# A longer weave of the gate stage, samples first in the query and key projections, and a later place for the attention output transposes

## The chip, the core and the metric

The kernel runs on one NeuronCore of one Trainium2 chip. The metric is the device time of one execution, in microseconds (us). Before the change three executions took 1855.73 us (median), 1855.55 us and 1857.43 us. The engines have short names here: PE is TensorE's matmul side and PEld its weight loads, DVE is VectorE, ACT is ScalarE, POOL is GpSimd, and SP is the engine that issues most DMAs.

## What is computed

The reference runs a small encoder of two layers over two batches that share their weights: a prompt of 512 tokens and a sample of 256 tokens, each 1024 wide.

```python
def _mixer(x, w_in, ...):
    aq, ak, av, lq, lk, lv, lo, lg = _split_cols(x @ w_in)
    att = _diff_attention(aq, ak, av, lam)            # 4 heads, two softmaxes each, ALiBi bias
    att = _head_rmsnorm(att, att_g) * (1.0 - lam_init)
    gates = lg + gate_bias                            # 16 columns: input and forget gates, two directions
    h_f = _mlstm_direction(q, k, v, ig_f, lf_f)       # chunks of 128 tokens, cumulative sums and running maxima
    h_b = flip(_mlstm_direction(flip(q), flip(k), flip(v), flip(ig_b), flip(lf_b)))
    lstm = sigmoid(lo) * _head_rmsnorm(h_f + h_b, lstm_g)
    return concatenate([att, lstm]) @ w_out
# each layer: x = LN1(ALPHA*x + mixer(x));  x = LN2(ALPHA*x + conv_gated_ffn(x))
```

## The kernel before

Both batches lie side by side as T = 768 tokens, in NT = 6 tiles of 128; tiles 0 and 1 are the sample (SB = 256 tokens), tiles 2 to 5 the prompt. A product in 32-bit accuracy is made of three passes: each operand is split into a high part and a rest, and high x high, high x rest and rest x high are summed in PSUM. So a projection of one token tile (`tok_major`) is 8 blocks of 128 inputs times three passes, 24 matmuls. The tiles of one projection are called after it: `av0` to `av5` (attention values), `lv0` to `lv5` (LSTM values), `lo0` to `lo5` (output gate).

Queries and keys of one head are made the other way round, features on the partitions (`feat_major`): 24 weight pieces, each used for the 256 sample columns (into the bank `aqkB`) and the 512 prompt columns (into `aqkA`). `att_in` does it twice per head, first for the query (`aqkA00` for head 0), then for the key (`aqkA01`). Both use the two halves of one sample bank (`aqkB0`). ACT and DVE then split the query into `sQ` and the key into `sK` and `kL`. `att` makes the scores (`s`), the two softmaxes and their difference (`tp`), its transpose (`aT`), the product with the values (`u`), and at the end of a batch the normalised output `ao` and its transpose `aoT`.

`gates` is a chain of small steps: logarithms of the gates, a transpose (`gT`), scans along the tokens on DVE (lines 483 to 487), maxima and exponentials, a small matmul that spreads a factor over the partitions (`aB`, line 517), and transposes back (`colT`). It also writes two scratch arrays to memory, from which `lstm_decay` later loads `pt` (512 KB, line 570) and `qet` by DMA. In `pt` DVE adds a mask (line 572) and ACT takes exponentials (line 574).

Weights come in pieces of 256 KB over the queue of SP (line 140). There are 6 buffers for them as they arrive, and 12 slots for the split form `wh`, `wl`, made by ACT (line 171) and DVE (line 172). A slot comes free when the last matmul that reads it is done, and a load waits until an older piece has been split.

The stages are generators. `weave` takes steps from several of them in turn, in the ratio of the numbers given with them, and so writes the program's order. Each instruction gets a priority from its place in that order; `prio(n)` shifts it, a negative n to a later place. A list scheduler then places each engine's instructions by priority, data and free buffers. In hardware each engine takes its list in order. `islice(lv, 1)` takes the first token tile from a projection and leaves the rest for later.

Of the kernel before, what the change touches and what calls it, by code (L numbers as in the profile page):

```python
# [20 lines left out]
SA, SB = 512, 256  # L21
T = SA + SB
# [24 lines left out]
PR_A = 0  # L47
PR_L = 0
PR_LO = 10
# [2 lines left out]
PR_S = -20  # L52
PR_T = -20
PR_E = 50
PR_CONV1 = -100
PR_CONV2 = -100
SBUFS = 2
# [148 lines left out]
def trunk(ctx, nc, tc, d, o, depth=DEPTH):  # L206
    V, S, G, PE = nc.vector, nc.scalar, nc.gpsimd, nc.tensor
# [11 lines left out]
    @contextmanager  # L219
    def prio(offset):  # L220

        tc.cur_priority -= offset
        yield
        tc.cur_priority += offset

    def P(tag, name):
        return pp.tile([128, 512], F32, tag=tag, name=name, bufs=banks[tag])

    actA = cp.tile([128, 8, 2, T], F32R, name="actA")
# [17 lines left out]
    for i in range(2):  # L247
        k = 4 * i
# [70 lines left out]
    ident = cp.tile([128, 128], F32, name="ident")  # L319
# [19 lines left out]
    PASSES = ((0, 0), (0, 1), (1, 0))  # L339

    def tok_major(t, blocks, ps, cols):

        for k, (_, h, l) in enumerate(blocks):
            for i, (a, b) in enumerate(PASSES):
                PE.matmul(ps, xh(k, t, a), (h, l)[b][:, cols], start=k + i == 0, stop=k == 7 and i == 2)  # L345

    def feat_major(blocks, psA, psB):

        n = 0
        for k in range(8):  # L350
            _, h, l = blocks[k // 4]
            for a, b in PASSES:
                w = (h, l)[a][:, (k % 4) * 128:(k % 4 + 1) * 128]
                PE.matmul(psB, w, actA[:, k, b, 0:SB], start=n == 0, stop=n == 23)  # L354
                PE.matmul(psA, w, actA[:, k, b, SB:T], start=n == 0, stop=n == 23)  # L355
                n += 1

    def transposed_split(src, name, tag, hi, lo):

# [8 lines left out]
    for l in range(depth):  # L368
# [3 lines left out]
        av = ra.tile([128, NT, 512], F32, name="av")  # L372
# [24 lines left out]
        def dense(tag, evac):  # L397
            units = [W.take() for _ in range(8)]
            for t in range(NT):
                p = P("d", f"{tag}{t}")  # L400
                tok_major(t, units, p, slice(0, 512))
                evac(t, p)
                yield
            W.done(*units)
# [23 lines left out]
        def gates():  # L428
# [38 lines left out]
            t2 = gp.tile([128, T], F32, name="t2")  # L467
            mpe = gp.tile([64, 2, 6], F32, name="mpe")
            ae = gp.tile([64, 6], F32, name="ae")
            for c0, c1 in ((0, 4), (4, 6)):  # L470
                ps = P(TAG_GT, f"gT{c0}")
                n = (c1 - c0) * 128
                for t in range(c0, c1):
                    PE.transpose(ps[:, (t - c0) * 128:(t - c0 + 1) * 128], gs[:, t].rearrange("p a b c -> p (a b c)"), ident)
                S.copy(ig[:, c0 * 128:c1 * 128], ps[0:64, :n])
                V.tensor_copy(lf[:, c0 * 128:c1 * 128], ps[64:128, :n])
# [35 lines left out]
            V.tensor_tensor(out=v6(t2[64:128]), in0=v6(t1[0:64]), in1=me.unsqueeze(2).to_broadcast([64, 6, 128]), op=ALU.subtract)  # L512
            V.tensor_tensor(out=ae, in0=mp, in1=me, op=ALU.subtract)
            S.activation(ae, ae, AF.Exp)
            ps = P(TAG_GT, "aB")
            for i in range(4):
                PE.matmul(ps[:, i * 6:(i + 1) * 6], sel[:, i, :], ae, start=True, stop=True)
# [2 lines left out]
            for c0, c1 in ((0, 4), (4, 6)):  # L520
                for ti, src in ((0, t1), (1, t2)):
                    ps = P(TAG_COLT[ti], f"colT{c0}{ti}")
# [169 lines left out]
        def att(h):  # L692
            slope = 2.0 ** (-8.0 * (h + 1) / 4)
            for s0, s1 in SEQ_ORDER[h]:
                nq = s1 - s0
                n = nq * 128
                keys = slice(s0 * 128, s1 * 128)
                pu = P("u", f"u{h}{s0}")
                ssu = sm.tile([128, 4], F32, tag="ssu", name=f"ssu{h}{s0}")
                sm0 = sm.tile([128, 4], F32, tag="sm0", name=f"sm0{h}{s0}")  # L700
                for qt in range(nq):
                    qtok = slice((s0 + qt) * 128, (s0 + qt + 1) * 128)
                    tp = ra.tile([128, 2, 512], F32, tag="tp", name=f"tp{h}{s0}{qt}", bufs=2)
                    mn = sm.tile([128, 2], F32, tag="mn", name=f"mn{h}{s0}{qt}")
                    cc = sm.tile([128, 1], F32, tag="cc", name=f"cc{h}{s0}{qt}")
                    for c in range(2):
                        ps = P("s", f"s{h}{s0}{qt}{c}")
                        PE.matmul(ps[:, :n], sQ[:, c, qtok], sK[:, c, keys], start=True, stop=False)
                        PE.matmul(ps[:, :n], sQ[:, c, qtok], kL[:, c, keys], start=False, stop=True)
                        V.tensor_tensor_reduce(out=tp[:, c, :n], in0=ps[:, :n], in1=dneg[:, 384 - 128 * qt:384 - 128 * qt + n], scale=-slope, scalar=3e38,  # L710
                                               op0=ALU.add, op1=ALU.min, accum_out=mn[:, c:c + 1])

                    for c in range(2):
                        S.activation(tp[:, c, :n], tp[:, c, :n], AF.Exp, bias=mn[:, c:c + 1], scale=-1.0, accum_out=sm0[:, qt:qt + 1] if c == 0 else cc)
                    V.reciprocal(cc, cc)
                    V.scalar_tensor_tensor(out=cc, in0=sm0[:, qt:qt + 1], scalar=nlam[:, l:l + 1], in1=cc, op0=ALU.mult, op1=ALU.mult)
                    V.scalar_tensor_tensor(out=tp[:, 0, :n], in0=tp[:, 1, :n], scalar=cc, in1=tp[:, 0, :n], op0=ALU.mult, op1=ALU.add)
                    pa = P(TAG_AT[qt % 2], f"aT{h}{s0}{qt}")
                    for st in range(nq):
                        PE.transpose(pa[:, st * 128:(st + 1) * 128], tp[:, 0, st * 128:(st + 1) * 128], ident)  # L720
                    aT = ra.tile([128, 512], F32, tag="aT", name=f"aT{h}{s0}{qt}", bufs=2)
                    CP[E_AT[qt % 2]](aT[:, :n], pa[:, :n])
                    for st in range(nq):
                        PE.matmul(pu[:, qt * 128:(qt + 1) * 128], aT[:, st * 128:(st + 1) * 128], av[:, s0 + st, h * 128:(h + 1) * 128], start=st == 0, stop=st == nq - 1)  # L724
                    S.activation(aT[:, 0:128], pu[:, qt * 128:(qt + 1) * 128], AF.Square, accum_out=ssu[:, qt:qt + 1])
                    yield

                V.scalar_tensor_tensor(out=sm0[:, :nq], in0=sm0[:, :nq], scalar=128 * EPS, in1=sm0[:, :nq], op0=ALU.mult, op1=ALU.mult)
                V.tensor_tensor(out=ssu[:, :nq], in0=sm0[:, :nq], in1=ssu[:, :nq], op=ALU.add)
                G.tensor_tensor(out=ssu[:, :nq], in0=ssu[:, :nq], in1=mhalf[:, 0:nq], op=ALU.pow)  # L730
                ao = ra.tile([128, 512], F32, tag="aT", name=f"ao{h}{s0}", bufs=2)
                V.tensor_tensor(out=ao[:, :n].rearrange("p (a b) -> p a b", b=128), in0=pu[:, :n].rearrange("p (a b) -> p a b", b=128),
                                in1=ssu[:, :nq].unsqueeze(2).to_broadcast([128, nq, 128]), op=ALU.mult)
                pt_ = P(TAG_AOT, f"aoT{h}{s0}")
                for qt in range(nq):
                    PE.transpose(pt_[:, qt * 128:(qt + 1) * 128], ao[:, qt * 128:(qt + 1) * 128], ident)
                S.activation(av[:, s0:s1, h * 128:(h + 1) * 128], pt_[:, :n].rearrange("p (a b) -> p a b", b=128), AF.Identity, scale=again[:, l, h:h + 1])

        def weave(*gens):

            live = [[0, n, i, g, (*o, 0)[0]] for i, (g, n, *o) in enumerate(gens)]
            while live:
                e = min(live, key=lambda e: ((e[0] + 0.5) / e[1], e[2]))
                e[0] += 1
                with prio(e[4]):
                    done = next(e[3], live) is live
                if done:
                    live.remove(e)

        def chain(*gens):  # L750
            for g in gens:
                yield from g
# [3 lines left out]
            late_constants()  # L756
        G.iota(dneg, [[-1, 896]], base=384, channel_multiplier=1, allow_small_or_imprecise_dtypes=True)
        V.scalar_tensor_tensor(out=dneg, in0=dneg, scalar=-1.0, in1=dneg, op0=ALU.mult, op1=ALU.min)
        weave((gates(), 8), (dense("av", ev_av), 7))
        CPX = ExitStack()  # L760
        lc = CPX.enter_context(tc.tile_pool(name=f"lc{l}", bufs=1, reuse_waits="tile"))
        weave((att_in(0), 3))
        weave((att(0), 7, PR_A), (dense("lv", ev_lv), 7, PR_LO))
        lo = dense("lo", ev_lo)
        weave((chain(att_in(1), att(1)), AT1, PR_A), (chain(lstm_states(lc), *[lstm_out(lc, c) for c in range(OUTS)]), 4 * OUTS + 9, PR_L), *([(islice(lo, L1), L1 + W1)] if L1 else []))
        weave((chain(att_in(2), att(2)), AT2, PR_A), (chain(*[lstm_out(lc, c) for c in range(OUTS, NT)]), 4 * (NT - OUTS) + 1, PR_L), *([(islice(lo, L2), L2 + W2, PR_LO)] if L2 else []))
# [36 lines left out]
        for t in range(NT):  # L803
            nc.sync.dma_start(acc[:, t, :], xres[t * 128:(t + 1) * 128])
        W.urgency = PR_CONV1
        LN = ExitStack()
# [200 lines left out]
        for i in range(FF_EARLY):  # L1007
            with prio(PR_E):
                next(started[i])
# [88 lines left out]
```

## Time and profile before

| | us |
|---|---|
| three executions | 1855.55, 1855.73, 1857.43 |
| profiled execution | 1855.45 |
| its span, first to last instruction | 1853.7 |
| PE busy | 1804.3 |
| DVE busy | 1340.4 |
| ACT busy | 768.9 |
| POOL busy | 241.9 |

The profiled execution is 1855.45 us long, its span 1853.7 us; 1.75 us lie outside the span. PE is busy for 97% of the span, so little is to be had but from its stops and from stretches in which its clock is low. The granted clock is shown as a share of full speed: 1.00 stands for 2.4 GHz and 0.50 for 1.2 GHz; a value between is a mean over a window. A timeline row says how long an engine stood idle before it and what released it. The end of a matmul is modelled, so that rows of matmuls overlap; the step from start to start is what one costs.

### The profile page before, as it was taken

What the parts mean: (1) busy time and instruction counts of PE and PEld (TensorE: products, weight loads), DVE (VectorE), ACT (ScalarE), POOL (GpSimd) and SP (SyncE); (2) the same over time, 40 slices, a digit from 0 to 9 for tenths busy, and PEclk for the clock granted to TensorE, in tenths of its full rate; (3) what the DMA queues carried; (4) which work ended last, traced back from release to release, by engine and by line L of the source; (5) the groups of instructions that cost most, each with busy time, mean ns of one, the idle gap of its engine ahead of it and who ended that gap; (6) DMA issues with size and microseconds to landing.
All of it is one profiled execution on the core that took longest, in us unless ns stands there. A gap on an engine that the chain in (4) does not pass through costs nothing.

```text
span 1853.7 us, 26256 instructions
## 1 busy us (share of the span) xinstructions
PE 1804.3 (97%) x9692; PEld 1587.1 (86%) x9692; DVE 1340.4 (72%) x2576; ACT 768.9 (41%) x1624; POOL 241.9 (13%) x260
## 2 busy tenths in 40 slices
PE   8899999999999999999998999999999999999998
PEld 8778777789899899899897787777898998998996
DVE  5434787589887786787954457775898877877878
ACT  4344576425343343343332455672353343343340
POOL 2000111041111111110120011011411111111102
PEclk9999999999999999999999999999999999999999
DMA  6232110402322222122322121104022221221211
GB/s 190 67 79 69 35 58 24 159 18 69 92 74 69 64 74 68 64 75 86 101 96 83 42 69 52 46 25 170 2 90 80 80 79 47 80 76 51 80 63 68
DMA packets 83280, 134.95 MB, mean 73 GB/s; under 512 B 7984, under 2 KB 27056, under 8 KB 83152
## 3 DMA queue, kind: packets, MB, share of 16 engines
q1 hardware_dynamic: 82432, 132.90, 22.7%
q8 instruction: 76, 1.25, 0.3%
q14 instruction: 52, 0.43, 0.1%
q10 hardware_dynamic: 720, 0.37, 0.1%
HBM read 126.86 MB, written 6.39 MB: 72 GB/s over the span
## 4 chain that ended last, share of the span: by engine, by line
PE 78%; DVE 13%; ACT 5%; issue 2%; POOL 2%; DMA 1%; SPq 0%; DVEq 0%; ACTq 0%; POOLq 0%
PE p L921 32%; PE dn L981 16%; PE wo L877 5%; PE aqkA L355 3%; PE lv L345 3%; PE lo L345 3%; PE aqkB L354 2%; DVE wl L172 2%; PE c1a L345 2%; PE u L724 2%; PE av L345 2%; PE c1b L345 2%; PE num L618 1%; ACT wh L171 1%; PE num L614 1%
## 5 line engine op out<-in xcount | busy, mean ns | idle before, releaser
L921 PE MATMUL p<-actA,wh 128*128 128x384 f32 x1408 | 363.4, 338 | 3.2 <-DVE g L946 3.2
L171 ACT ACTIVATE wh<-raw 128x512 fp32r<-128x512 f32 (+1 forms) x348 | 215.5, 629 | 303.3 <-PE p L921 110.2
L172 DVE TENSOR_TENSOR wl<-raw,wh 128x512 fp32r<-128x512 f32 (+1 forms) x348 | 243.2, 708 | 96.9 <-ACT wh L171 96.4
L921 PE MATMUL p<-actB,wh 128*128 128x384 f32 x1056 | 270.0, 337 | 0.0
L921 PEld LDWEIGHTS p<-actA,wh 128*128 128x128 f32 x1408 | 254.7, 188 | 5.8 <-DVE g L946 3.8
L921 PE MATMUL p<-actA,wl 128*128 128x384 f32 x704 | 237.3, 337 | 0.0
L149 POOL TENSOR_TENSOR T<-raw,raw 128x512 f32<-128x512 f32 x88 | 120.5, 1371 | 837.0 <-DVE wl L172 525.7
L981 PE MATMUL dn<-wh,actB 128*128 128x512 f32 x576 | 208.8, 396 | 1.1 <-DVE acc L988 1.1
L171 ACT ACTIVATE wh<-T 128x512 fp32r<-128x512 f32 x176 | 108.4, 628 | 221.3 <-DVE acc L988 104.9
L921 PEld LDWEIGHTS p<-actB,wh 128*128 128x128 f32 x1056 | 191.3, 188 | 0.0
L981 PE MATMUL dn<-wh,ring 128*128 128x512 f32 x480 | 179.1, 396 | 1.6 <-DVE acc L988 1.6
L921 PE MATMUL p<-actB,wl 128*128 128x384 f32 x528 | 177.2, 336 | 0.0
L988 DVE TENSOR_TENSOR acc<-acc,dn 128x512 f32<-128x512 f32 x144 | 98.1, 681 | 72.0 <-PE dn L981 71.7
L172 DVE TENSOR_TENSOR wl<-T,wh 128x512 fp32r<-128x512 f32 x176 | 129.6, 748 | 22.0 <-ACT wh L171 21.9
L981 PEld LDWEIGHTS dn<-wh,actB 128*128 128x128 f32 x576 | 108.0, 188 | 29.8 <-DVE acc L988 2.8
L921 PEld LDWEIGHTS p<-actA,wl 128*128 128x128 f32 x704 | 132.2, 188 | 0.1
L877 PE MATMUL wo<-wh,actB 128*128 128x512 f32 x384 | 122.7, 396 | 0.0
L981 PE MATMUL dn<-wl,actB 128*128 128x512 f32 x288 | 113.2, 393 | 0.0
L981 PEld LDWEIGHTS dn<-wh,ring 128*128 128x128 f32 x480 | 90.0, 188 | 24.6 <-DVE acc L988 4.2
L921 PEld LDWEIGHTS p<-actB,wl 128*128 128x128 f32 x528 | 99.1, 188 | 0.0
L355 PE MATMUL aqkA<-actA,wh 128*128 128x512 f32 x256 | 98.8, 408 | 0.0
L981 PE MATMUL dn<-wl,ring 128*128 128x512 f32 x240 | 94.5, 394 | 0.0
(265 smaller groups left out, 3412.5 us busy)
## 6 DMA issues: line engine op xcount, KB each, us to landing
raw<-in_w_g_dram SPq DMA_DIRECT2D x88, 256.0 KB, 2.8
raw<-in_w_u_dram SPq DMA_DIRECT2D x88, 256.0 KB, 2.8
raw<-in_w_down_dram SPq DMA_DIRECT2D x88, 256.0 KB, 2.8
raw<-in_w_out_dram SPq DMA_DIRECT2D x32, 256.0 KB, 2.6
pt<-scr_m SPq DMA_DIRECT2D x12, 512.0 KB, 6.2
raw<-in_w_c_dram SPq DMA_DIRECT2D x16, 264.0 KB, 3.6
raw<-in_w_av_dram SPq DMA_DIRECT2D x16, 256.0 KB, 4.1
raw<-in_w_aq_dram SPq DMA_DIRECT2D x16, 256.0 KB, 3.7
```

The source lines that it names most:

```text
L149: src["engine"].tensor_tensor(out=src["tile"], in0=a, in1=b, op=ALU.subtract)
L171: self.nc.scalar.activation(h, v, AF.Identity)
L172: self.nc.vector.tensor_tensor(out=l, in0=v, in1=h.bitcast(F32), op=ALU.subtract)
L345: PE.matmul(ps, xh(k, t, a), (h, l)[b][:, cols], start=k + i == 0, stop=k == 7 and i == 2)
L354: PE.matmul(psB, w, actA[:, k, b, 0:SB], start=n == 0, stop=n == 23)
L355: PE.matmul(psA, w, actA[:, k, b, SB:T], start=n == 0, stop=n == 23)
L614: PE.matmul(pn[:, di * 256:di * 256 + 129], qet[r, di, hh // 2, :], cst[di, c][r, hh // 2, :], start=di == dirs[0], stop=False, skip_group ...
L724: PE.matmul(pu[:, qt * 128:(qt + 1) * 128], aT[:, st * 128:(st + 1) * 128], av[:, s0 + st, h * 128:(h + 1) * 128], start=st == 0, stop=st ...
L877: PE.matmul(p, actB[:, k, a, t * 128:(t + 1) * 128], units[k][1 + b], start=n + i == 0, stop=n == 7 and i == 2)
L921: PE.matmul(ps, blk[1 + a][:, k * 128:(k + 1) * 128], x[:, k, b, :], start=k + i == 0, stop=k == 3 and i == 2)
L981: PE.matmul(p, x, (wh_, wl_)[b], start=k + i == 0, stop=k == nf - 1 and i == 2)
L988: V.tensor_tensor(out=z, in0=z, in1=p, op=ALU.add)
```

## The change

The change has three parts. The gate stage gets two more places at which the weave may take another stage's step, and is woven with a longer list: the value projection, then the whole query and key projection of head 0, then the first tile of the LSTM value projection; before, it was woven with the value projection alone, and the projection of head 0 came after it. In `feat_major` all 24 matmuls of the sample columns come first and then all 24 of the prompt columns, in place of one each in turn. And the transposes `aoT` get a priority shift to a later place. The number of instructions of each kind is the same.

```diff
--- before.py
+++ after.py
@@ -52,6 +52,7 @@
 PR_S = -20
 PR_T = -20
 PR_E = 50
+PR_AO = -40
 PR_CONV1 = -100
 PR_CONV2 = -100
 SBUFS = 2
@@ -346,14 +347,14 @@
 
     def feat_major(blocks, psA, psB):
 
-        n = 0
-        for k in range(8):
-            _, h, l = blocks[k // 4]
-            for a, b in PASSES:
-                w = (h, l)[a][:, (k % 4) * 128:(k % 4 + 1) * 128]
-                PE.matmul(psB, w, actA[:, k, b, 0:SB], start=n == 0, stop=n == 23)
-                PE.matmul(psA, w, actA[:, k, b, SB:T], start=n == 0, stop=n == 23)
-                n += 1
+        for ps, tok in ((psB, slice(0, SB)), (psA, slice(SB, T))):
+            n = 0
+            for k in range(8):
+                _, h, l = blocks[k // 4]
+                for a, b in PASSES:
+                    w = (h, l)[a][:, (k % 4) * 128:(k % 4 + 1) * 128]
+                    PE.matmul(ps, w, actA[:, k, b, tok], start=n == 0, stop=n == 23)
+                    n += 1
 
     def transposed_split(src, name, tag, hi, lo):
 
@@ -467,6 +468,7 @@
             t2 = gp.tile([128, T], F32, name="t2")
             mpe = gp.tile([64, 2, 6], F32, name="mpe")
             ae = gp.tile([64, 6], F32, name="ae")
+            yield
             for c0, c1 in ((0, 4), (4, 6)):
                 ps = P(TAG_GT, f"gT{c0}")
                 n = (c1 - c0) * 128
@@ -512,6 +514,7 @@
             V.tensor_tensor(out=v6(t2[64:128]), in0=v6(t1[0:64]), in1=me.unsqueeze(2).to_broadcast([64, 6, 128]), op=ALU.subtract)
             V.tensor_tensor(out=ae, in0=mp, in1=me, op=ALU.subtract)
             S.activation(ae, ae, AF.Exp)
+            yield
             ps = P(TAG_GT, "aB")
             for i in range(4):
                 PE.matmul(ps[:, i * 6:(i + 1) * 6], sel[:, i, :], ae, start=True, stop=True)
@@ -732,8 +735,9 @@
                 V.tensor_tensor(out=ao[:, :n].rearrange("p (a b) -> p a b", b=128), in0=pu[:, :n].rearrange("p (a b) -> p a b", b=128),
                                 in1=ssu[:, :nq].unsqueeze(2).to_broadcast([128, nq, 128]), op=ALU.mult)
                 pt_ = P(TAG_AOT, f"aoT{h}{s0}")
-                for qt in range(nq):
-                    PE.transpose(pt_[:, qt * 128:(qt + 1) * 128], ao[:, qt * 128:(qt + 1) * 128], ident)
+                with prio(PR_AO):
+                    for qt in range(nq):
+                        PE.transpose(pt_[:, qt * 128:(qt + 1) * 128], ao[:, qt * 128:(qt + 1) * 128], ident)
                 S.activation(av[:, s0:s1, h * 128:(h + 1) * 128], pt_[:, :n].rearrange("p (a b) -> p a b", b=128), AF.Identity, scale=again[:, l, h:h + 1])
 
         def weave(*gens):
@@ -756,11 +760,11 @@
             late_constants()
         G.iota(dneg, [[-1, 896]], base=384, channel_multiplier=1, allow_small_or_imprecise_dtypes=True)
         V.scalar_tensor_tensor(out=dneg, in0=dneg, scalar=-1.0, in1=dneg, op0=ALU.mult, op1=ALU.min)
-        weave((gates(), 8), (dense("av", ev_av), 7))
+        lv = dense("lv", ev_lv)
+        weave((gates(), 10), (chain(dense("av", ev_av), att_in(0), islice(lv, 1)), 10))
         CPX = ExitStack()
         lc = CPX.enter_context(tc.tile_pool(name=f"lc{l}", bufs=1, reuse_waits="tile"))
-        weave((att_in(0), 3))
-        weave((att(0), 7, PR_A), (dense("lv", ev_lv), 7, PR_LO))
+        weave((att(0), 7, PR_A), (lv, 6, PR_LO))
         lo = dense("lo", ev_lo)
         weave((chain(att_in(1), att(1)), AT1, PR_A), (chain(lstm_states(lc), *[lstm_out(lc, c) for c in range(OUTS)]), 4 * OUTS + 9, PR_L), *([(islice(lo, L1), L1 + W1)] if L1 else []))
         weave((chain(att_in(2), att(2)), AT2, PR_A), (chain(*[lstm_out(lc, c) for c in range(OUTS, NT)]), 4 * (NT - OUTS) + 1, PR_L), *([(islice(lo, L2), L2 + W2, PR_LO)] if L2 else []))
```

The first place is PE in the gate stage of layer 0. The rows show the matmul `aB` with its neighbours; `av2` and `av3` are tiles of the value projection. Before:

```order
L345 MATMUL av2_784<-wl25_573,actA_70 128x512
L345 MATMUL av2_784<-wh25_572,actA_70 128x512
L345 MATMUL av2_784<-wh26_578,actA_70 128x512
L517 MATMUL aB_778<-ae_686,sel_636 128x6 x4
L345 MATMUL av2_784<-wl26_579,actA_70 128x512
L345 MATMUL av2_784<-wh26_578,actA_70 128x512
```

And now:

```order
L346 MATMUL av3_804<-wh28_590,actA_70 128x512
L346 MATMUL av3_804<-wl28_591,actA_70 128x512
L346 MATMUL av3_804<-wh28_590,actA_70 128x512
L520 MATMUL aB_830<-ae_686,sel_636 128x6 x4
L346 MATMUL av4_836<-wh21_188,actA_70 128x512
L346 MATMUL av4_836<-wl21_189,actA_70 128x512
```

Before, 64 matmuls of the value projection stood ahead of `aB` (67 in layer 1); now 96 do, in both layers.

The second place is ACT at the projection of head 0, in layer 0: `wh` is a weight split, `sQ` takes the query out of PSUM, `pt0` is the exponential on data that come by DMA, `tp` the softmax of the first scores. Before:

```order
L171 ACTIVATE wh41_1012<-raw41_926 128x512
L574 ACTIVATE pt0_1834<-pt0_1834,cols_239 128x128 x5
L678 ACTIVATE sQ_228<-aqkB0_962 64x256
L679 ACTIVATE sQ_228<-aqkB0_962 64x256
L678 ACTIVATE sQ_228<-aqkA00_963 64x512
L679 ACTIVATE sQ_228<-aqkA00_963 64x512
L171 ACTIVATE wh42_1018<-raw42_932 128x512
```

And now, first where `sQ` is made and then where `pt0` stands:

```order
L681 ACTIVATE sQ_228<-aqkB0_949 64x256
L682 ACTIVATE sQ_228<-aqkB0_949 64x256
L172 ACTIVATE wh41_999<-raw41_917 128x512
L172 ACTIVATE wh42_1005<-raw42_923 128x512
L681 ACTIVATE sQ_228<-aqkA00_950 64x512
L682 ACTIVATE sQ_228<-aqkA00_950 64x512
```

```order
L577 ACTIVATE pt0_1834<-pt0_1834,cols_239 128x128 x5
L413 COPY vaug_237<-lv0_1101 128x4x128
L577 ACTIVATE pt0_1834<-pt0_1834,cols_239 128x128
L717 ACTIVATE tp000_1135,sm000_1134<-tp000_1135,mn000_1136 128x256
L717 ACTIVATE tp000_1135,cc000_1137<-tp000_1135,mn000_1136 128x256
L577 ACTIVATE pt0_1834<-pt0_1834,cols_239 128x128 x2
L577 ACTIVATE pt1_1856<-pt1_1856,cols_239 128x128 x7
L725 COPY aT000_1154<-aT000_1151 128x256
```

The five exponentials of `pt0` stood ahead of `sQ`; now they stand behind all of `sQ` and `sK`, and ahead of the first softmax `tp000`.

The third place is DVE at the first scores of head 0, in layer 0: L710 before and L713 now reduce the scores, `kL` is the rest of the key, L572 and L575 add the mask to `pt`. Before:

```order
L710 ISA tp000_1108,mn000_1109<-s0000_1111,dneg_233 128x256
L710 ISA mn000_1109 128x1
L710 ISA tp000_1108,mn000_1109<-s0001_1115,dneg_233 128x256
L710 ISA mn000_1109 128x1
L687 TENSOR_TENSOR kL_230<-aqkA01_1032,sK_229 64x512
L688 TENSOR_TENSOR kL_230<-aqkA01_1032,sK_229 64x512
L715 RECIPROCAL cc000_1110<-cc000_1110 128x1
L716 SCALAR_TENSOR_TENSOR cc000_1110<-sm000_1107,nlam_221,cc000_1110 128x1
L717 SCALAR_TENSOR_TENSOR tp000_1108<-tp000_1108,cc000_1110 128x256
```

And now:

```order
L575 TENSOR_TENSOR pt0_1834<-pt0_1834,tri_243 128x512 x2
L713 ISA tp000_1135,mn000_1136<-s0000_1138,dneg_233 128x256
L713 ISA mn000_1136 128x1
L713 ISA tp000_1135,mn000_1136<-s0001_1142,dneg_233 128x256
L713 ISA mn000_1136 128x1
L575 TENSOR_TENSOR pt1_1856<-pt1_1856,tri_243 128x512
L718 RECIPROCAL cc000_1137<-cc000_1137 128x1
L575 TENSOR_TENSOR pt1_1856<-pt1_1856,tri_243 128x512
L719 SCALAR_TENSOR_TENSOR cc000_1137<-sm000_1134,nlam_221,cc000_1137 128x1
```

Between the first scores and the first difference `tp000` stood the rest of the key; now the masks of `pt0` stand ahead of these scores and those of `pt1` among them. In SP's list the load of `pt0` now stands three weight loads further back, behind the first load for `lo`, which waits until block 43 (`wh43`, `wl43`), a piece of the key weights of head 1, has been split.

## Rows read from the trace of the kernel before

**Rows 1.** The page: busy time of TensorE, and of its weight loads.

```profile
PE 1804.3 (97%) x9692; PEld 1587.1 (86%) x9692; DVE 1340.4 (72%) x2576; ACT 768.9 (41%) x1624; POOL 241.9 (13%) x260
```

**Rows 2.** Waits of PE in the whole span: total us, times, longest us.

```profile
PE aB L517 <- ACT ae L514: 10.5, 2, 5.3
PE aqkB L354 <- DVE sQ L681: 5.8, 2, 3.4
PE p L921 <- DVE g L946: 3.2, 2, 1.6
```

**Rows 3.** Timeline of PE: start, us, instruction, count, idle before and its releaser.

```profile
45.19 0.40 PE L345 MATMUL av<-wh,actA 128*128 128x512 f32 x1
50.55 0.63 PE L474 MATMUL gT<-ident,gs 128*128 128x128 f32 x4 [0.80 <-DVE gs L461]
67.11 1.84 PE L517 MATMUL aB<-ae,sel 64*128 64x6 f32 x8 [5.26 <-ACT ae L514]
966.81 0.39 PE L345 MATMUL av<-wh,actA 128*128 128x512 f32 x1
973.25 0.63 PE L474 MATMUL gT<-ident,gs 128*128 128x128 f32 x4 [1.16 <-DVE gs L461]
989.80 1.84 PE L517 MATMUL aB<-ae,sel 64*128 64x6 f32 x8 [5.25 <-ACT ae L514]
```

**Rows 4.** Windows: length, busy by engine (count), TensorE clock granted, DMA share, GB/s.

```profile
67.00:73.00 6.00, 5.89 (x19) 5.02 (x20) 0.18 (x1) 0.31 (x1) 0.00 (x0) 0.51 0.02 5
989.00:995.00 6.00, 5.20 (x19) 4.58 (x20) 0.18 (x1) 1.40 (x4) 0.00 (x0) 0.54 0.02 4
425.00:450.00 25.00, 23.38 (x134) 23.06 (x133) 23.40 (x38) 13.28 (x22) 5.98 (x4) 1.00 0.23 76
```

**Rows 5.** The chain that ended last: start, us, what.

```profile
24.91 2.85 PE c1b L345 x24
73.28 5.55 PE av L345 x24
93.04 7.22 DMA pt<-scr_m
1014.60 6.18 DMA pt<-scr_m
```

**Rows 6.** Timeline of PE at the second projection pass of head 0, both layers.

```profile
104.34 0.79 PE L354 MATMUL aqkB<-actA,wh 128*128 128x256 f32 x2 [3.43 <-DVE sQ L681]
1024.81 0.51 PE L354 MATMUL aqkB<-actA,wh 128*128 128x256 f32 x2 [2.37 <-DVE sQ L681]
```

**Rows 7.** Windows behind those two stops.

```profile
104.00:111.00 7.00, 6.66 (x25) 5.95 (x26) 4.25 (x7) 4.31 (x13) 0.00 (x0) 0.54 0.15 40
1024.00:1030.00 6.00, 5.19 (x23) 4.70 (x24) 4.47 (x8) 3.70 (x9) 0.00 (x0) 0.72 0.18 55
```

**Rows 8.** Timeline of ACT from 101 to 122 us.

```profile
101.16 1.57 ACT L574 ACTIVATE pt<-pt,cols 128x128 f32<-128x128 f32 x5 [5.72 <-DVE pt L572]
113.81 0.63 ACT L171 ACTIVATE wh<-raw 128x512 fp32r<-128x512 f32 x1 [2.04 <-PE aqkA L355]
118.27 0.51 ACT L714 ACTIVATE tp<-tp,mn 128x256 f32<-128x256 f32 x1
121.56 0.59 ACT L412 COPY vaug<-lv 128x512 f32<-128x512 f32 x1
```

**Rows 9.** Timeline of DVE from 100 to 121 us.

```profile
100.39 1.29 DVE L572 TENSOR_TENSOR pt<-pt,tri 128x512 f32<-128x512 f32 x2 [4.22 <-DMA pt<-scr_m]
114.48 0.69 DVE L172 TENSOR_TENSOR wl<-raw,wh 128x512 fp32r<-128x512 f32 x1 [4.28 <-ACT wh L171]
120.28 0.48 DVE L717 SCALAR_TENSOR_TENSOR tp<-tp,cc 128x256 f32<-128x256 f32 x1
```

**Rows 10.** Waits of PE from 125 to 340 us.

```profile
PE cu L553 <- ACT cst L557: 0.3, 1, 0.3
```

**Rows 11.** Weight loads of the sample passes, 90 to 100 us: mean ns of one.

```profile
L354 PEld LDWEIGHTS aqkB<-actA,wh 128*128 128x128 f32 x16 | 3.0, 189 | 0.0
```

## The prediction

> **What bounds the kernel now.** I read the page first, then the waits of PE, then the timeline of PE around the longest of them, then the windows behind these stops, and last what ACT, DVE and the DMAs do there.
>
> PE is busy for 1804.3 us [rows 1], so about 49 us of the span are its stops. Two waits of PE are long and come once in each layer: `aB` for ACT, 10.5 us in two stops, and `aqkB` for DVE, 5.8 us in two [rows 2]. Both lie in the stages that the change touches.
>
> The first stop is in the gate stage. PE has given out its 64 (layer 1: 67) matmuls of the value projection and waits for `aB`, 5.26 and 5.25 us [rows 3]. What it waits for is a chain on DVE and ACT that nothing disturbs. The clock falls with the stop: in the 6 us behind it the granted clock is 0.51 and 0.54, for 5.89 and 5.20 us of busy PE [rows 4]. So the stop costs twice. A small stop at `gT`, 0.80 and 1.16 us, stands ahead of it [rows 3].
>
> The second stop is between query and key of head 0, 3.43 and 2.37 us [rows 6]. The key needs the sample bank, which the query's evictions still hold. These stand in ACT's list behind five exponentials of `pt0` [rows 8], those wait for DVE's mask, and that waited 4.22 us for the load of `pt0` [rows 9], 7.22 us long in layer 0 and 6.18 in layer 1 [rows 5]. Behind these stops the clock is 0.54 over 6.66 us busy and 0.72 over 5.19 us [rows 7].
>
> **The first stop, part by part.** Now 96 matmuls stand ahead of `aB`. 24 of them take 5.55 us [rows 5], 0.231 us each. Layer 0: from 45.19 us [rows 3], 96 x 0.231 = 22.2 and some 0.6 for the six `gT` transposes make 68.0 us. The chain was ready at 67.1 [rows 3]. `gT` now starts after all 24 matmuls of `av0`, at 50.75 in place of 50.55, and its copy stands behind that of `av0` on ACT, so I add 0.3: ready at 67.4, 0.6 us before PE arrives. Layer 1: `gT` starts at 973.25 as before, for its data set that; 72 matmuls (16.6 us) and 0.5 for transposes make 990.4 against 989.8. The stop goes in both layers, though with little to spare. A chain late by 1 us would cost 0.4 us.
>
> What goes: stops of 5.26 and 5.25 us; the low clock, 5.89 x 0.49 = 2.89 us and 5.20 x 0.46 = 2.39 us; at `gT` 0.80 us and, by the two matmuls more ahead of it, 0.46 us. Together 17.05 us. What PE does in that time is work taken from later (the rest of the value projection, then head 0), so the work behind it comes earlier, and the question is what is late next.
>
> **The second stop.** `sQ` of the sample now stands ahead of all `pt0` work in ACT's list, and the key's sample pass begins only after the query's prompt pass, 24 x 0.231 = 5.5 us later. Evicting the sample query takes some 2 us, with a split of 0.63 us in front [rows 8]. So both stops go: 3.43 + 2.37, and the low clock, 6.66 x 0.46 = 3.06 and 5.19 x 0.28 = 1.45. Together 10.31 us. All removed: 27.36 us.
>
> The new order inside a pass I cost at nothing. 24 sample matmuls in a row, each with its own weights, cost 2.85 us where `c1b` does just this [rows 5], 0.119 us each. With 0.231 for a prompt matmul a pair is 0.350, about what a pair costs in the alternating order. Over the 384 pairs of the kernel each 0.01 us would be 3.8 us.
>
> On this the Trainium skill, "TensorE: Matmul & The Clock Gate", section "Step-by-step: what each phase is for", speaks against the change: weights are loaded on their own so that one load can serve many matmuls, and the old order put the two matmuls with equal weights next to each other. By that rule the change would add 384 loads. The trace before has as many weight loads as matmuls, 9692 each [rows 1], so none was shared, and none is added.
>
> **What is late next.** The `pt0` wait has moved. In ACT's list it stands before the first softmax of head 0, and on DVE before and among the reductions of its scores. I count from the end of the key's prompt pass, t = 0. Block 43 can be split when half of that pass is done, t = -2.8; ACT 0.63 [rows 8] and DVE 0.69 [rows 9] make -1.3. Then SP issues the load for `lo`, then `pt0`, at -0.9. With 6.18 to 7.22 us [rows 5], less traffic in front of it now, it lands at 5.3 to 6. Two masks, 1.29 us [rows 9], end at 6.6 to 7.3; the two reductions of the scores behind them end 0.8 us later. On ACT five exponentials (1.57), the eviction of `lv0` (0.59) [rows 8] and one more exponential follow the first mask, to 8.5 to 9.3; the two softmaxes (from 0.51 each, 1.1 with their sums) [rows 8] end at 9.6 to 10.4. DVE must put in a mask of `pt1` on either side of the reciprocal, 0.65 each, and then the mix (0.48) [rows 9]: `tp000` is ready at 11.7 to 12.4. PE arrives at its transpose after `colT` (0.3), `lv0` (5.55), four score matmuls (0.5) and 16 of `lv1` (3.7), t = 10.1. So I expect a new stop there of 1.6 to 2.3 us, 1.8 taken.
>
> ACT still has nine exponentials of `pt0` and `pt1` to do around the copy that follows; I put 0.7 us on the next two steps. Will the clock fall? It did at 2.37 us [rows 6]; at the stop of 1.6 us on `g` [rows 2] it stayed at 1.00 [rows 4]. 1.8 is nearer to that, so I charge nothing, at the other end 1.45 us.
>
> At the start of head 1 the last key pass now lies closer to the scores. Four evictions of the prompt key hold DVE until 4.4 us after that pass, and PE has about 3 us of other work ahead of what needs it. Before, the stop there was 0.3 us [rows 10]. I take 1.4 us, between 0 and 3.
>
> The later place of `aoT` I cost at nothing: its stops are among the small waits of the attention stage, and the last ones, before the output projection, stand in nearly the same place. It could give or cost 0.5 us in each layer.
>
> **Sum.** New: 1.8 + 0.7 + 1.4 = 3.9 us a layer, 7.8 in all. 27.4 - 7.8 = 19.6 us. Against the profiled execution's 1855.45 us (span 1853.7, 1.75 outside; median of the runs 1855.73) this makes 1835.9 us.
>
> **Rivals.**
> 1. The moved wait costs as the old one did. The stop before `tp000` grows to that of layer 1, 2.37 with 1.45 of low clock, or to that of layer 0, 3.43 with 3.06. For it: the same load, issued behind one more wait. Against: fewer loads ahead of it. With 2.1 for the rest of a layer, 27.4 - 2 x (3.82 + 2.1) = 15.6 gives 1839.9; 27.4 - 2 x (6.49 + 2.1) = 10.2 gives 1845.2.
> 2. Nothing new is late. `pt0` lands in 4 us and head 1 runs as before; 0.5 us a layer is left: 1829.1. For it: DMA is otherwise idle then. Against: both loads seen took over 6 us [rows 5].
> 3. The change does not do what it says for the gate stage: the chain is delayed by as much as PE is filled. Then the 15.8 us of the first stop stay, and 1851.7 is the result. Against: the chain's list on DVE is unchanged.
> 4. Slower. The sample passes become bound by their weight loads. A load is shown as 189 ns [rows 11], and in the new order 0.119 us of matmul stand over each, where before a prompt matmul stood between. If each of 384 sample matmuls took 0.189, that is 0.07 x 384 = 26.9 us more: 1862.8. It decides from 0.17 us per matmul (19.6 / 384 = 0.05 above 0.119). Against: `c1b` runs 24 such in 2.85 us with its own loads.
>
> **Numbers.** Forecast (1831 to 1839) 0.55, rival 1 0.22, rival 2 0.12, rival 3 0.05, rival 4 0.04, and 0.02 for a cause I do not see. 1828 to 1847 holds the first three, about 0.85; I leave 3 and 4 outside. About 0.2%, 3.7 us, is what a measurement of this kernel tells from no change. Faster by more: 0.92; within it: 0.04 (half of rival 3, what is not seen); slower: 0.04.
>
> **What would show it.** PE waits no longer for `aB` and `aqkB`; the windows behind have a clock of 1.00; the time from the first `av0` matmul to the first of `aqkB0` is some 36 us in place of 45.4. A new wait of `aT` for DVE of about 2 us a layer, with `pt` masks waiting for the DMA in front of it. The sample passes take 2.85 us for 24. I am wrong if `aB` still waits over 1 us, if the stop at `aT` exceeds 2.4 us and brings the low clock, if a pass of 24 exceeds 3.5 us, or if head 1 and later heads have stops of more than 3 us together in a layer.

## The result and the profile after

The changed kernel took 1832.35 us (median of four executions, 1831.11 to 1833.44) against 1856.58 us before (four executions, 1855.55 to 1857.58): a ratio of 0.9869, 95% interval 0.9852 to 0.9886. Forecast were 1835.9 us and a range of 1828 to 1847. The profiled execution took 1831.93 us, 23.5 us less than the one before; the forecast was 19.6 less.

The page after, its row of busy time; before, [rows 1]:

```profile
PE 1796.4 (98%) x9692; PEld 1580.8 (86%) x9692; DVE 1345.2 (74%) x2576; ACT 768.2 (42%) x1624; POOL 241.8 (13%) x260
```

The waits of PE after (total us, times, longest us) answer to [rows 2]:

```profile
PE c1a L346 <- ACT actA L172: 7.2, 1, 7.2
...
PE aoT L740 <- DVE ao L735: 2.6, 4, 1.0
PE aT L723 <- DVE tp L720: 2.5, 2, 1.4
```

`aB` (10.5 us) and `aqkB` (5.8 us) are gone from the list; the wait for the first input, 7.2 us, was there before too, with 7.7 us. New is `aT`, 2.5 us. The timeline of PE in layer 0 after, which answers to [rows 3, 6]:

```profile
45.65 0.40 PE L346 MATMUL av<-wh,actA 128*128 128x512 f32 x1
51.21 0.60 PE L476 MATMUL gT<-ident,gs 128*128 128x128 f32 x4
68.67 1.05 PE L520 MATMUL aB<-ae,sel 64*128 64x6 f32 x8
...
110.25 0.44 PE L723 MATMUL aT<-ident,tp 128*128 128x128 f32 x2 [1.42 <-DVE tp L720]
...
155.27 0.63 PE L740 MATMUL aoT<-ident,ao 128*128 128x128 f32 x4 [1.03 <-DVE ao L735]
```

PE comes to `aB` at 68.67, and no bracket stands there: it does not wait. ACT had finished `ae` a little earlier, as its timeline shows:

```profile
67.42 0.21 ACT L516 ACTIVATE ae<-ae 64x6 f32<-64x6 f32 x1
```

So the 96 matmuls cover the chain with 68.67 - 67.63 = 1.04 us to spare (0.6 was forecast); in layer 1 it is 978.15 - 977.05 = 1.10 us.

From the first value matmul to the first `wo` matmul a layer takes 275.96 and 276.66 us. Two windows, from the first `av` to the first `wo` of each layer, split this (length, busy PE and its count, granted clock, DMA share, GB/s). Before:

```profile
45.19:334.46 289.27, 276.81 (x1518) 0.98 0.19 57
966.81:1253.64 286.83, 275.12 (x1518) 0.98 0.19 57
```

After:

```profile
45.65:321.61 275.96, 271.21 (x1518) 1.00 0.19 59
954.20:1230.86 276.66, 271.53 (x1519) 1.00 0.19 58
```

The layers lose 13.31 and 10.17 us, together 23.48; everything else in the program differs by 0.1 in sum. Idle time falls from 12.46 and 11.71 to 4.75 and 5.13 us, which is 14.29 us less. Busy time falls by 5.60 and 3.59, which is 9.19 us less for the same matmuls: that is, in the main, the low clock, which [rows 4, 7] put at 9.79 us.

### The profile page after: what moved, and what is told of

It is laid out like the page before. It is cut to its first block, busy times and chain, and to the rows that moved or that the text cites. A ratio compares the mean times of both kernels' runs of the same rounds, so it can differ in the third digit from the quotient of the medians.

```text
span 1830.1 us, 26254 instructions
## 1 busy us (share of the span) xinstructions
PE 1796.4 (98%) x9692; PEld 1580.8 (86%) x9692; DVE 1345.2 (74%) x2576; ACT 768.2 (42%) x1624; POOL 241.8 (13%) x260
## 4 chain that ended last, share of the span: by engine, by line
PE 81%; DVE 11%; ACT 2%; POOL 2%; issue 2%; DMA 1%; SPq 0%; DVEq 0%; POOLq 0%; ACTq 0%
PE p L925 32%; PE dn L985 16%; PE wo L881 5%; PE aqkA L356 4%; PE av L346 3%; PE lo L346 3%; PE lv L346 3%; PE aqkB L356 2%; DVE wl L173 2%; PE u L727 2%; PE c1a L346 2%; PE c1b L346 2%; PE num L621 1%; PE num L617 1%; PE s L711 1%
## 5 line engine op out<-in xcount | busy, mean ns | idle before, releaser
L881 PEld LDWEIGHTS wo<-wh,actB 128*128 128x128 f32 x384 | 71.8, 188 | 16.2
```

The source lines that it names most:

```text
L881: PE.matmul(p, actB[:, k, a, t * 128:(t + 1) * 128], units[k][1 + b], start=n + i == 0, stop=n == 7 and i == 2)
```

## The experiments

Each was run beside the kernel before; the quoted text was written ahead of the run.

**e1, the gate weave alone.** The changed kernel with the loop of `feat_major` and the place of `aoT` as before:

```diff
-        for ps, tok in ((psB, slice(0, SB)), (psA, slice(SB, T))):
...
-                    PE.matmul(ps, w, actA[:, k, b, tok], start=n == 0, stop=n == 23)
+                PE.matmul(psB, w, actA[:, k, b, 0:SB], start=n == 0, stop=n == 23)
+                PE.matmul(psA, w, actA[:, k, b, SB:T], start=n == 0, stop=n == 23)
...
-                with prio(PR_AO):
```

> The longer gate weave alone (alternating sample and prompt columns and the old place of aoT, as in the kernel before). Theory: the stop at aB and its low clock go in both layers, 17.05 us. At head 0 the pt0 work now stands behind the query's evictions, but an alternating pass ends its sample half as late as its prompt half, so the key's first sample matmul still waits for two ACT and two DVE evictions of 0.4 us each: a stop of 1.5 to 2 us a layer at aqkB with the clock at 1.00, in place of 3.43 and 2.37 with a low clock. So 1832.35 + 2 x 1.8 = 1836 us. Rival 1: the order inside the pass has a price of its own (0.01 us a pair is 3.8 us), then 1832 or less with the same stop. Rival 2: the weave does not help the second stop, it stays at 2.4 to 3.4 us with its low clock: 1842 us.

Measured: 1832.24 us, ratio 0.9868 (0.9853 to 0.9883). The whole gain comes from the weave. My time was 4 us too long: there is no stop of 1.5 to 2 us. In layer 1 it is 0.39 us, in layer 0 none, as the timeline of PE at the seam of the two passes shows:

```profile
89.87 0.70 PE L356 MATMUL aqkA<-actA,wh 128*128 128x512 f32 x2
...
91.93 0.51 PE L355 MATMUL aqkB<-actA,wh 128*128 128x256 f32 x2
...
1001.22 0.50 PE L355 MATMUL aqkB<-actA,wh 128*128 128x256 f32 x2 [0.39 <-DVE sQ L684]
```

The scheduler itself sends eight prompt matmuls of the key ahead (89.87 to 91.7) while the sample bank is being emptied. I had read the order as strictly alternating.

The trace holds one thing more: the stop at `aT` is smaller here, 0.40 and 0.54 us against 1.42 and 1.00 in the changed kernel, since the mask of `pt1` on DVE waits less for its load. DVE and PE:

```profile
106.79 0.69 DVE L575 TENSOR_TENSOR pt<-pt,tri 128x512 f32<-128x512 f32 x1 [0.31 <-DMA pt<-scr_m]
```

```profile
109.10 0.44 PE L723 MATMUL aT<-ident,tp 128*128 128x128 f32 x2 [0.40 <-DVE tp L720]
```

So samples first, added to the weave, is not without effect: it takes away the 0.39 us at `aqkB` and 0.3 us a layer at a later wait of the scores for `sK` (0.9 to 0.6), and brings more at `aT` (in e3, where it is the only difference from e1, 1.6 and 1.1 us). Over both layers PE's idle time is 9.76 us in e1 and 9.88 us in the changed kernel.

**e2, samples first alone**, on the kernel before:

```diff
-                PE.matmul(psB, w, actA[:, k, b, 0:SB], start=n == 0, stop=n == 23)
-                PE.matmul(psA, w, actA[:, k, b, SB:T], start=n == 0, stop=n == 23)
+        for ps, tok in ((psB, slice(0, SB)), (psA, slice(SB, T))):
...
+                    PE.matmul(ps, w, actA[:, k, b, tok], start=n == 0, stop=n == 23)
```

> Samples first alone, on the kernel before. Theory: the stop at aB stays at 5.2 us a layer with a clock near 0.5 behind it; the stop at aqkB goes (3.43 and 2.37 with 3.06 and 1.45 of low clock, 10.3 us), because the query's sample eviction stands ahead of the pt0 exponentials; but these still stand ahead of the key's sample eviction, so a stop of 0 to 1.5 us a layer comes at the first scores: 1846 to 1849 us. A pass of 24 sample matmuls takes 2.8 to 2.9 us. Rival 1: the part needs the longer weave, since pt0 still holds ACT: 1854 to 1857 us. Rival 2: the sample passes are bound by their weight loads, 0.07 us for each of 384 matmuls: slower than 1870 us.

Measured: 1851.27 us, ratio 0.9967 (0.9954 to 0.9979), 2 us beyond what I expected. The stop at `aqkB` goes, that at `aB` stays, and a new one comes one step later than I had it, at `aT`. PE's timeline:

```profile
68.35 1.84 PE L517 MATMUL aB<-ae,sel 64*128 64x6 f32 x8 [5.26 <-ACT ae L514]
...
117.21 0.44 PE L720 MATMUL aT<-ident,tp 128*128 128x128 f32 x2 [2.18 <-DVE tp L717]
...
1035.40 0.44 PE L720 MATMUL aT<-ident,tp 128*128 128x128 f32 x2 [2.12 <-DVE tp L717]
```

On ACT the query's sample eviction now stands ahead of the exponentials of `pt0`, since the sample bank is full earlier:

```profile
95.73 0.38 ACT L678 ACTIVATE sQ<-aqkB 64x256 fp32r<-64x256 f32 x1 [1.76 <-PE aqkB L355]
...
103.12 0.99 ACT L574 ACTIVATE pt<-pt,cols 128x128 f32<-128x128 f32 x3 [4.13 <-DVE pt L572]
```

Samples first helps a kernel that lacks the weave; it is another way to the gain that the weave already has at the second stop, and it too brings `sQ` ahead of `pt0`.

**e3, the old place of `aoT`** in the changed kernel:

```diff
-                with prio(PR_AO):
-                    for qt in range(nq):
+                for qt in range(nq):
```

> The changed kernel with aoT at its old place. Theory: the third part is worth nothing that can be told, 1832.4 us within 1 us, and the stop of 1.0 us at aoT in front of the second half of the head 1 query stays, since the transposes stand in the same place there. Rival: the later place causes that stop; without it 1830.3 us. Other rival: the later place saved 2 to 4 us: 1835 us.

Measured: 1832.57 us, 0.9869 (0.9855 to 0.9882). The third part is worth nothing that can be told, and the stop of 1.05 us at `aoT` stays:

```profile
156.44 0.63 PE L739 MATMUL aoT<-ident,ao 128*128 128x128 f32 x4 [1.05 <-DVE ao L735]
```

**e4, 24 matmuls fewer ahead of `aB`.**

```diff
-        weave((gates(), 10), (chain(dense("av", ev_av), att_in(0), islice(lv, 1)), 10))
+        weave((gates(), 10), (chain(dense("av", ev_av), att_in(0), islice(lv, 1)), 7))
```

> The changed kernel with ratio 10 to 7 in place of 10 to 10 in the gate weave: 72 value matmuls stand ahead of aB in place of 96, the same instructions otherwise. Theory: PE comes to aB 5.55 us earlier than in the changed kernel, where it came 1.04 us after ae was done, so a stop of 4.5 us in each layer, and a low clock behind it that costs 2.4 to 2.9 us more: 1832.35 + 2 x 7.1 = 1846.6 us. Rival 1: the low clock is not the stop's doing: 1841.4 us. Rival 2: the gain of the first part came from head 0 and not from aB: 1832 to 1834 us.

Measured: 1846.05 us, 0.9940 (0.9927 to 0.9952). Timeline of PE at `aB`:

```profile
68.02 1.62 PE L520 MATMUL aB<-ae,sel 64*128 64x6 f32 x8 [4.60 <-ACT ae L516]
...
984.34 1.84 PE L520 MATMUL aB<-ae,sel 64*128 64x6 f32 x8 [4.54 <-ACT ae L516]
```

And the windows behind these stops (columns as in [rows 4]):

```profile
68.00:74.00 6.00, 5.98 (x18) 5.03 (x19) 0.18 (x1) 0.35 (x1) 0.00 (x0) 0.52 0.02 5
984.30:990.30 6.00, 5.96 (x19) 5.11 (x20) 0.18 (x1) 0.36 (x1) 0.00 (x0) 0.54 0.02 4
```

Two stops of 9.14 us together make the kernel 13.7 us longer. The rest is the low clock: 5.98 x 0.48 + 5.96 x 0.46 = 5.6 us, which gives 14.7, less 1.5 us at `aT`, where the two stops are now 0.28 and 0.61: 13.2. That a stop costs twice is shown.

**e5, the gate stage alone.** Two `yield`s and ratio 10 to 10, but woven with the value projection only:

```diff
-        weave((gates(), 8), (dense("av", ev_av), 7))
+        weave((gates(), 10), (dense("av", ev_av), 10))
```

> The kernel before with only the two more places in the gate stage and the ratio 10 to 10 with the value projection; the projection of head 0 and the LSTM values follow as before, alternating, aoT as before. Theory: the first stop and its low clock go (17.05 us), the second stays, since seven exponentials of pt0 still stand ahead of the query's eviction on ACT: a stop of 2.4 to 4 us a layer at aqkB with a low clock behind it, 1857.2 - 17 = 1840 us (1838 to 1842). Rival 1: the weave with the value projection is all there is in the change: 1832 us. Rival 2: the chain of gates comes out later for the two more places: 1845 us or more.

Measured: 1839.04 us, 0.9906 (0.9893 to 0.9920). The first stop is worth 17.0 us, as forecast. The second stays: PE's timeline, and the windows behind it.

```profile
96.16 0.50 PE L355 MATMUL aqkB<-actA,wh 128*128 128x256 f32 x2 [3.75 <-DVE sQ L684]
...
1008.49 0.63 PE L355 MATMUL aqkB<-actA,wh 128*128 128x256 f32 x2 [3.33 <-DVE sQ L684]
```

```profile
96.10:103.10 7.00, 6.94 (x34) 6.15 (x35) 3.46 (x6) 3.75 (x11) 0.00 (x0) 0.76 0.23 75
1008.00:1015.00 7.00, 6.51 (x31) 5.97 (x32) 3.88 (x6) 4.17 (x12) 0.00 (x0) 0.76 0.19 62
```

By the working of the prediction the second stop costs what it did before, 10.3 us (3.75 + 3.33, and 6.94 x 0.24 + 6.51 x 0.24 of low clock), so the 17.0 us are the first stop's alone. So it is the head's own projection in the weave that removes the second stop: it moves the pass ahead of the `pt0` work.

**e6, the load of `pt1` held back** in the changed kernel until head 0 is done:

```diff
+            if c == 1:
+                S.copy(pt[:, 0, 0, 0:1], av[:, 5, 0:1])
             nc.sync.dma_start(pt.rearrange("p a b j -> p (a b) j"), ...)
```

> The changed kernel, where the load of pt1 waits for the end of head 0 (a copy of one column of av into pt1 ahead of the load, overwritten by it; one small copy a layer more). Theory: the stop at aT000 (1.42 and 1.00 us) comes from the mask of pt1, which stands ahead of the reciprocal on DVE and waits for a load of 6.3 us; held back, the stop falls below 0.4 us, and the work behind comes earlier: 1832.35 - 2 = 1830 to 1831 us; up to 1 us a layer may come back at the first scores of head 1, where the mask now stands. Rival: pt0, its masks and its exponentials make the stop; it stays at 1.0 us or more, 1832 us.

Measured: 1830.81 us, 0.9862 (0.9849 to 0.9876), which by time alone does not stand apart from the changed kernel. The trace does: the two stops at `aT` fall from 1.42 and 1.00 to 0.42 and 0.39 us, though four matmuls fewer now stand ahead of the transpose.

```profile
108.03 0.44 PE L725 MATMUL aT<-ident,tp 128*128 128x128 f32 x2 [0.42 <-DVE tp L722]
...
1015.96 0.44 PE L725 MATMUL aT<-ident,tp 128*128 128x128 f32 x2 [0.39 <-DVE tp L722]
```

**e7, `pt0` and `pt1` held back in the kernel before**, with nothing of the change:

```diff
+            if c < 2:
+                S.copy(pt[:, 0, 0, 0:1], av[:, 5, 0:1])
```

> The kernel before, where the loads of pt0 and pt1 wait for the end of head 0 (the same copy). Nothing of the change is in it. Theory: the second stop is made by pt0 ahead of the query's evictions on ACT alone, and not by the order of the columns: without pt0 there ten prompt matmuls of the key (2.3 us) cover the two evictions of about 0.4 us on ACT and two on DVE, the stop at aqkB falls below 0.5 us, and its low clock goes: 1857.2 - 10.3 = 1847 us, up to 2 us a layer more where pt comes late at head 1. Rival: the alternating order holds the bank too, a stop of 2 us a layer stays: 1852 us.

Measured: 1853.98 us, 0.9982 (0.9973 to 0.9991). In head 0 the stop at `aqkB` is gone in both layers: `pt0` made it, and not the order of the columns. But it comes again at the second pass of head 1, where `pt` now stands ahead of the query's evictions. PE's timeline there, and the windows behind:

```profile
170.15 0.51 PE L354 MATMUL aqkB<-actA,wh 128*128 128x256 f32 x2 [2.89 <-DVE sQ L683]
...
1090.01 0.74 PE L354 MATMUL aqkB<-actA,wh 128*128 128x256 f32 x2 [2.70 <-DVE sQ L683]
```

```profile
170.10:177.10 7.00, 6.96 (x41) 6.05 (x41) 2.76 (x4) 5.22 (x17) 0.00 (x0) 1.00 0.22 75
1090.00:1097.00 7.00, 7.00 (x33) 6.31 (x34) 2.74 (x4) 5.09 (x16) 0.00 (x0) 0.76 0.16 58
```

My time, 1847 us with up to 2 us a layer more, was too short: the mechanism held at its place, and I had mis-sized what comes late next.

**e8, `aoT` later still:**

```diff
-PR_AO = -40
+PR_AO = -80
```

> The changed kernel with the shift of aoT at -80 in place of -40. Theory: the stops of 1.03 and 1.02 us at aoT in the query pass of head 1 go, as 9 to 10 more matmuls stand ahead of it, and nothing waits for its result there: 1830.3 us. Rival: the late result holds a buffer of the attention of head 0 or 1, and stops of the same size come elsewhere: 1832 us or more.

Measured: 1829.14 us, 0.9854 (0.9839 to 0.9869). The wait of `aoT` for `ao` falls from 2.6 us in the changed kernel to 0.5. From PE's waits:

```profile
PE aT L723 <- DVE tp L720: 1.9, 2, 1.2
...
PE aoT L740 <- DVE ao L735: 0.5, 2, 0.3
```

Over the two layers PE's idle time is 7.53 us against 9.88 in the changed kernel, and its busy time 541.54 us against 542.74. So a third of what the trace gains is busy time, for the same matmuls.

**e9, e6 and e8 together.**

> The changed kernel with both edits: the load of pt1 held until the end of head 0, and the shift of aoT at -80. Theory: the two gains are of different stops (aT000 in head 0; aoT in the query pass of head 1) and add: against the changed kernel's 1832.35 us some 1.5 from the first and 3.2 from the second, 1827.7 us, and no stop of PE over 0.9 us between the value projection and the output projection. Rival: what the one edit wins, the other had won already, since a late step is caught up at the next stop: 1829 us.

Measured: 1829.17 us, 0.9854 (0.9836 to 0.9872). The rival's time came, but not for its reason. The stops at `aT` are 0.43 and 0.40 us, as in e6, and no stop grows in their place: idle time over both layers is 6.56 us, against 9.88 in the changed kernel, 8.19 in e6 and 7.53 in e8. By their sum 5.84 was to be had, so the stops add in the main. What does not add is busy time. Head 1 begins 0.35 us earlier after the first value matmul than in e8 (98.33 against 98.68 us), and the first layer is 0.42 us longer all the same (274.20 against 273.78): PE is busy for 271.23 us in it, 270.64 in e8. Layer 1 of e8 and of e9 (length, busy PE, granted clock, DMA share, GB/s):

```profile
951.77:1227.06 275.29, 270.91 (x1518) 1.00 0.19 59
```

```profile
952.64:1227.86 275.22, 271.63 (x1518) 1.00 0.19 59
```

The 1.2 us of busy time that e8 is shorter by is not found in e9, at the same granted clock and for the same matmuls (one profiled execution of each). Why stays open.

The medians of e6, e8 and e9 are 1.5 to 3.2 us below that of the changed kernel; their intervals overlap its own. The four executions of e8 (1828.14 to 1829.26) all lie below the four of the changed kernel (1831.11 to 1833.44), but were not made side by side: that e8 beats the change is likely, and not shown.

## Why the prediction was right

**The first stop: right in size and cause.** 17.05 us were forecast, 17.0 came in e5, where this is the only edit. Layer 0 kept 1.04 us to spare, and `gT` of layer 1 kept 0.69 us of its stop, 0.47 less, where 0.46 was forecast.

**The second stop: right in size; one of two reasons is shown.** Both stops and their low clock went. I gave two reasons, `sQ` ahead of `pt0` and the key's sample pass after a whole prompt pass. The first is enough without the second (e1 but for 0.39 us in layer 1, e7). The second was not tested without the first: samples first without the weave (e2) takes the stop away, with 4.3 us of new stops at `aT`, but brings `sQ` ahead of `pt0` as well. To the time of the weave it adds nothing.

**The order inside a pass costs nothing.** The chain after has 24 sample matmuls and 24 prompt matmuls of the query and of the key:

```profile
81.92 2.81 PE aqkB L356 x24
84.73 5.54 PE aqkA L356 x24
90.49 2.85 PE aqkB L356 x24
```

2.81 and 2.85 us for 24, as `c1b` has in [rows 5]; rival 4 would have needed 4.1 us. The weight loads are 9692 before and after. The rule of the Trainium skill, "TensorE: Matmul & The Clock Gate", section "Step-by-step: what each phase is for", on one load that serves many matmuls, has no hold here, since no load was shared.

**What is late next: the term that was mis-sized.** 7.8 us were forecast for both layers. With 17.58 us of stops gone (9.49 and 8.09) and idle time less by 14.29, the new stops cost 3.29. The stop at `aT` is 1.42 and 1.00 us, 1.8 forecast, without a low clock, as forecast. But its maker is another one, and that the size came near is luck: I had `pt0` land 5.3 to 6 us after the key's pass and hold masks, reductions and softmaxes. The chain of waits after shows what ended last:

```profile
98.74 0.64 ACT wh L172
...
99.40 0.70 DVE wl L173
...
100.12 0.33 SPq L141
...
100.50 0.69 SPq L580
...
101.88 6.29 DMA pt<-scr_m
...
108.19 0.69 DVE pt L575
```

That is the load of `pt1`: issued behind a weight piece that waits for DVE's split, and behind two loads of `qet`. DVE's timeline shows the same:

```profile
103.20 1.29 DVE L575 TENSOR_TENSOR pt<-pt,tri 128x512 f32<-128x512 f32 x2
...
108.19 0.69 DVE L575 TENSOR_TENSOR pt<-pt,tri 128x512 f32<-128x512 f32 x1 [2.48 <-DMA pt<-scr_m]
108.80 0.16 DVE L718 RECIPROCAL cc<-cc 128x1 f32<-128x1 f32 x1
```

The masks of `pt0` (103.20) wait for nothing: its load took 4.2 us, where I had 6.18 to 7.22 from [rows 5]. The view of the tile has it:

```profile
DMA to landing us min/median/max: 4.2/4.2/4.2
```

The mask of `pt1` waits 2.48 us, ahead of the reciprocal on which `tp000` hangs; e6 shows that it makes most of the stop, and e1, where the mask waits 0.31 us, agrees. The 0.7 us for the next two steps did not come. The 1.4 us at the start of head 1 did not come at the scores; a stop of 1.03 and 1.02 us stands shortly before, at `aoT`. The later place of `aoT`, which I had costed at nothing, does not make it: it is 1.02 us in e1 and 1.05 us in e3, both without that edit. In sum 7.8 - 3.29 = 4.5 us too much, against 0.6 too much for the low clock (9.79 forecast, 9.19 measured): the 3.9 us between 19.6 and 23.5. A new load ahead of a short chain was the right place to look; which of two loads, and how long it takes with other traffic, was not to be had from the load of the stage before.

**The signs.** `aB` and `aqkB` wait no more, and from the first `av0` matmul to the first of `aqkB0` it is 81.67 - 45.65 = 36.02 us, as forecast. One of the four signs of being wrong came by its letter: from the first projection of head 1 to the first `wo` PE is idle for 3.34 and 3.39 us, over the 3 us that I had set. But the kernel before has 2.63 and 2.67 us there, which the bound left out of account; 0.7 us a layer is new, where 1.4 was forecast.

## What to carry to other kernels

When an engine waits for a long chain of small steps elsewhere, count the independent matmuls that stand ahead of the wait and put in as many as the chain is long: 32 more removed 5.26 us of waiting and 2.9 us of low clock. A load whose first use is placed too early in an in-order engine's list holds everything behind it, and moving the load moves the stop (e7); look at what stands behind it. Test each part of a change alone: here one of three had the whole gain.

## What was not expected of the hardware

The length of a stop alone did not tell whether the clock falls. Behind stops of 2.12, 2.18 (e2) and 2.89 us (e7, first layer) the granted clock was 1.00 over the next 7 us; behind 2.37 [rows 7], 2.70 (e7, second layer) and 3.33 us (e5) it was 0.72, 0.76 and 0.76 over 6 to 7 us. The windows of e2:

```profile
117.20:124.20 7.00, 6.99 (x37) 5.53 (x38) 2.14 (x9) 2.65 (x10) 0.00 (x0) 1.00 0.00 1
1035.40:1042.40 7.00, 7.00 (x37) 5.53 (x38) 2.14 (x9) 2.65 (x10) 0.00 (x0) 1.00 0.00 1
```

The 0.76 of e7 is a mean; right behind the stop the clock is near the level of 1.2 GHz, and from 1094 us on it is 1.00:

```profile
1090.00:1092.00 2.00, 2.00 (x9) 2.00 (x10) 1.96 (x3) 1.98 (x7) 0.00 (x0) 0.53 0.11 33
```

What decides it stays open. The eleven executions of e7, with two stops of this length, lie between 1849.32 and 1856.38 us, and their mean granted clock goes with the time: 0.996 and 0.995 in the two shortest, 0.993 in the two longest. So the low clock seems to come in some of them and not in others; at which stop is not shown, since one execution was profiled.

The same load of 512 KB took 4.2 us for `pt0` and 6.29 us for `pt1`, 4.16 us later in the same queue, with loads of `qet` on either side of the second.
